# Value projections of a hybrid GLA/mLSTM layer with the weights held and the tokens streamed, turned back through a DRAM scratch

## The chip, the cores and the metric

The kernel runs on one core of a Trainium2 chip. The metric is the device time of one execution in microseconds (us), the median of three runs. The profile is that of one execution. TensorE (PE in the profile) multiplies: it holds a stationary tile of 128 x 128 and streams columns of the moving operand past it; VectorE (DVE), ScalarE (ACT) and GpSimd (POOL) work on tiles in on-chip memory; SyncE (SP) issues most DMA transfers, in the order of its program.

## The reference, cut to what matters

One decoder layer on 1024 tokens of width 1024, with 16 meta tokens ahead of them. The mixing block projects the normed tokens, runs four GLA heads and four mLSTM heads in chunks of the sequence, and merges the two; a gated, convolved FFN follows. The change touches `g_v` and `m_v`, the values of the heads: 1040 tokens x 256 columns for each head.

```python
proj = h @ w_in + b_in
g_q, g_k, g_v, g_r, g_lr, m_q, m_k, m_v, m_o, ... = split(proj)
# per head and chunk, GLA:
out   = (q * exp(bc)) @ S + scores @ vc
S_new = exp(b_last) * S + (k * exp(b_last - bc)).T @ vc
# mLSTM: num = w_inter * (qc @ C) + qk @ vc ; C_new = g_prev * C + (w_state * k).T @ vc
```

## The kernel before, in words

**Precision and tiles.** The normed tokens lie in on-chip memory with the model dimension on the partitions, as `xH` and `xL` (128 x 8 blocks x 1040 tokens each; rounded part and remainder). Each weight unit comes from DRAM as a raw tile `wr_*` by a SyncE DMA (`prep`, L131 to L148) and is split into `wH_*` (ScalarE copy, L146) and `wL_*` (VectorE subtract, L147). Two raw tiles and three pairs of split ones are there at a time, so a weight load waits until an earlier raw tile has been split. The split is held behind a named instruction (`hold`), so that it doesn't come ahead of an eviction. A product is three matmuls per block of 128: H x H, H x L, L x H.

**Keys, queries and merge gates** (`proj_cm`, matmul L234) hold the weights and stream tokens, in thirds of some 346 columns (342 for gates), and leave output columns on the partitions and tokens along the free dimension.

**Values** (`value_proj`, `proj_v`, L247 to L281) are wanted the other way round: `vt` (128 x 9 x 257) has tokens on the partitions, one group for the meta tokens and one for each of the eight chunks of 128. So the tokens are the stationary operand, and the weights stream, 256 columns at a time; a head's weights come as two units of four blocks x 256 columns (1 KB runs). Each head has nine PSUM tiles `pv` (of the ring `pj`, three banks, which keys, queries and gates use too): the meta tile, 16 matmuls with the packed `xM` (meta columns of `xH` and `xL` side by side, L263), joined by a ScalarE copy (L268) and VectorE adds (L269, L270); then eight chunks of 24 matmuls (L276), each evicted by one VectorE add of a bias spread over the partitions, `bB` (L280; loaded per head by SyncE, L598).

**Who uses `vt`.** In `gla` (heads 0 to 3) and `mlstm` (4 to 7): the states `u` (L1004, L1128) and `up` (L997, L1124), the meta output `omp` (L1014, L1140), and the output `op` (L1038, L1156). `up{s}_{c}` uses chunk c+1 of `vt` (for GLA, pairs of chunks). When a head is done, `post` scales and turns its output by VectorE block transposes (L750) into tiles `of` of the ring `r` (two buffers) and stores them by SyncE in four pieces each to the scratch `oscg` or `oscm` (L760).

**The order of the work.** `main` (L1193) walks the projections of the heads as generators, and after each step lets the side work (the attention of the head before, `gla(s)` or `mlstm(s)`, then `post`) go on by 1.15 steps: key and query of head 0, then for each head s its values, then the keys and queries of head s+1. A value projection has nine steps. Behind the last head come three merge gates (units gb0 to gb2, tiles pj33 to pj35), during which head 7 is finished; then two more gates (gb3, gb4, tiles `pc`) on other banks, and then the gate products `Vg`, `Xg`, `Yg`, `Zg` (L1222), with operands from `TL`, tiles that SyncE loads from the scratch `tsc` (L1337) behind the stores of head 7. `gw00`, `gw10` and so on are weights for later. A scheduler with priorities turns the program's order into an order for each engine; that is fixed when the kernel is built.

## Time and profile before

| | |
|---|---|
| median of three runs | 1838.67 us (1837.76 to 1839.79) |
| the profiled execution: its time, its span | 1838.8 us, 1837.1 us |
| granted TensorE clock | 0.998 |
| busy: TensorE, VectorE, ScalarE, GpSimd | 1820.4, 1243.0, 850.6, 442.7 us |
| value projections on TensorE start at | 67.0, 122.3, 189, 254.2, 321.4, 377.5, 441.9, 512.7 us |
| end of the last value projection, of head 7 | 542.1, 564.3 us |

How to read it: the span is from the first to the last instruction of the profiled execution. A row of a group ends in "xcount | busy us, mean ns of one | idle time of the engine just before them, and what ended most of it". A row of the chain has its start, its duration, the engine, the tile's name without its number, the line and the count. The profile names lines of the kernel before; those of the kernel after are a few to some twenty higher.

### The profile page before, as it was taken

The numbers are of one execution on the slowest core, as the hardware profiler recorded it, in microseconds if no ns is written. First come the engines' busy times: TensorE is split into PE (matmuls) and PEld (weight loads), VectorE is DVE, ScalarE is ACT, GpSimd is POOL, SyncE is SP. The second block draws the span as 40 slices with busy tenths as digits, with TensorE's granted clock in tenths as the row PEclk, the third lists the DMA queues.
The fourth block names the chain that finished last, engine by engine and source line by source line (L and its number), as shares of the span: only waits on it lengthen the run. The fifth ranks groups of instructions, "written<-read, shape, count | busy, mean of one in ns | idle before, by whom it ended". The sixth has DMA issues, their size and how long they took to land.

```text
span 1837.1 us, 32479 instructions
## 1 busy us (share of the span) xinstructions
PE 1820.4 (99%) x13142; PEld 1754.7 (96%) x13142; DVE 1243.0 (68%) x1858; ACT 850.6 (46%) x1366; POOL 442.7 (24%) x511
## 2 busy tenths in 40 slices
PE   8999999999999999999999999999999999999998
PEld 7999999999999999999999999999999999988876
DVE  7966856656553666764614537798878887787776
ACT  6564564645444433422512335544434434465664
POOL 6400211105530011134462710022222222200010
PEclk9999999999999999999999999999999999999999
DMA  5211212224436354566964743344333343398794
GB/s 164 59 48 52 55 31 61 57 74 141 127 81 180 87 169 152 161 186 197 341 195 130 255 143 128 106 125 121 104 110 109 105 129 114 98 340 314 279 381 163
DMA packets 237469, 269.63 MB, mean 147 GB/s; under 512 B 15282, under 2 KB 194797, under 8 KB 237319
## 3 DMA queue, kind: packets, MB, share of 16 engines
q1 hardware_dynamic: 215583, 196.20, 34.3%
q0 software_dynamic: 19136, 62.62, 9.9%
q10 hardware_dynamic: 2600, 8.74, 1.3%
q8 instruction: 103, 1.69, 0.4%
q14 instruction: 47, 0.39, 0.1%
HBM read 197.91 MB, written 69.60 MB: 146 GB/s over the span
## 4 chain that ended last, share of the span: by engine, by line
PE 87%; DVE 6%; DMA 3%; ACT 2%; issue 2%; POOL 1%; SPq 0%; POOLq 0%; DVEq 0%; ACTq 0%
PE pj L234 10%; PE pv L276 8%; PE Yu L1222 7%; PE Zu L1222 7%; PE Xu L1222 7%; PE bg L1475 5%; PE bm L1475 5%; PE Zg L1222 4%; PE Yg L1222 4%; PE Xg L1222 4%; PE po L1769 4%; PE Vu L1222 3%; PE pdZ L1925 2%; PE pdX L1925 2%; PE pdY L1925 2%; PE Vg L1222 2%
## 5 line engine op out<-in xcount | busy, mean ns | idle before, releaser
L657 POOL TENSOR_TENSOR ts<-ts 128x256 f32<-128x256 f32 x88 | 80.0, 916 | 47.9 <-DMA ts<-in_ffn_w_down_dram 46.1
L1682 POOL TENSOR_TENSOR SB<-SA,rg 128x512 f32<-128x512 f32 x20 | 32.8, 1638 | 239.5 <-issue 101.4
L276 PE MATMUL pv<-wH_mv,xH 128*128 128x256 f32 x256 | 74.5, 291 | 0.1
L276 PE MATMUL pv<-wH_gv,xH 128*128 128x256 f32 x256 | 74.3, 290 | 0.0
L1769 PE MATMUL po<-wH_wo,yH 128*128 128x256 f32 x256 | 72.5, 283 | 0.1
L276 PE MATMUL pv<-wH_gv,xL 128*128 128x256 f32 x256 | 72.0, 281 | 0.0
L276 PE MATMUL pv<-wL_mv,xH 128*128 128x256 f32 x256 | 72.0, 281 | 0.0
L1769 PE MATMUL po<-wL_wo,yH 128*128 128x256 f32 x256 | 71.7, 281 | 0.3 <-DVE wL_wo L147 0.3
L276 PE MATMUL pv<-wL_gv,xH 128*128 128x256 f32 x256 | 71.9, 281 | 0.0
L276 PE MATMUL pv<-wH_mv,xL 128*128 128x256 f32 x256 | 71.9, 281 | 0.0
L1769 PE MATMUL po<-wH_wo,yL 128*128 128x256 f32 x256 | 71.8, 281 | 0.0
L1717 DVE SCALAR_TENSOR_TENSOR cv<-u,fc,cv 128x1024 f32<-128x1024 f32 x44 | 65.2, 1481 | 0.4
L1664 POOL TENSOR_TENSOR A<-u2raw,A 128x512 fp32r<-128x512 f32 x20 | 42.5, 2124 | 86.2 <-ACT A L1663 86.2
L924 POOL TENSOR_TENSOR pk<-pk,kT 128x256 f32<-128x256 f32 (+1 forms) x24 | 31.8, 1330 | 130.2 <-ACT pk L922 130.2
L1475 PE MATMUL bg<-ogL,wH_bg 128*128 128x342 f32 x192 | 61.5, 320 | 0.0
L1475 PE MATMUL bg<-ogH,wH_bg 128*128 128x342 f32 x192 | 61.5, 320 | 0.0
L1475 PE MATMUL bm<-omH,wH_bm 128*128 128x342 f32 x192 | 61.4, 320 | 0.0
L1475 PE MATMUL bm<-omH,wL_bm 128*128 128x342 f32 x192 | 61.3, 319 | 0.0
L1475 PE MATMUL bg<-ogH,wL_bg 128*128 128x342 f32 x192 | 61.3, 319 | 0.0
L1475 PE MATMUL bm<-omL,wH_bm 128*128 128x342 f32 x192 | 61.2, 319 | 0.0
L280 DVE TENSOR_TENSOR v<-pv,bB 128x256 f32<-128x256 f32 x64 | 26.6, 415 | 40.0 <-PE pv L276 39.8
L1663 ACT ACTIVATE HA<-rg 128x1024 fp32r<-128x1024 f32 x16 | 17.0, 1060 | 72.7 <-PE Yu L1222 72.3
(829 smaller groups left out, 7479.6 us busy)
## 6 DMA issues: line engine op xcount, KB each, us to landing
gw<-in_w_in_dram SPq DMA_DIRECT2D x26, 512.0 KB
ts<-in_ffn_w_down_dram POOLq DMA_DIRECT2D x44, 256.0 KB, 4.4
tdn<-ts POOLq DMA_DIRECT2D x44, 256.0 KB, 3.3
rg<-in_ffn_w_up_dram SPq DMA_DIRECT2D x22, 512.0 KB
ru<-in_ffn_w_up_dram SPq DMA_DIRECT2D x22, 512.0 KB
adr<-s SPq DMA_DIRECT2D x40, 256.0 KB
rd<-in_ffn_w_down_dram SPq DMA_DIRECT2D x20, 512.0 KB
do<-tdn SPq DMA_DIRECT2D x18, 512.0 KB
```

What stands on the lines that cost most here:

```text
L234: nc.tensor.matmul(pt[:, :n], a[:, k, :], b[:, k, base + t0:base + t0 + n], start=(i == 0), stop=(i == 3 * NK - 1))
L276: nc.tensor.matmul(pt[:, :DV], a[:, k, t0:t0 + P], b[:, k % 4, :], start=(i == 0), stop=(i == 3 * NK - 1))
L280: hold(nc.vector.tensor_tensor(vt[:n, c, :DV], pt[:n, :DV], bB[:n, :], OP.add).ins)
L657: nc.gpsimd.tensor_tensor(t[:, o], t[:, a], t[:, b], OP.subtract)
L924: eng.tensor_tensor(e, e, k, OP.mult)
L1222: nc.tensor.matmul(out[:, :n], x[:, k, :], y[:, k, :], start=start and k == 0 and j == 0, stop=stop and k == 3 and j == 2, skip_group_chec ...
L1475: nc.tensor.matmul(pt[:, i, :n], a[:, k, :], b[k][:, base + t0:base + t0 + n], start=(k == 0 and j == 0), stop=(k == NK - 1 and j == 2))
L1664: eng.tensor_tensor(l, src, h.bitcast(F32), OP.subtract)
L1682: late.tensor_tensor(sb[:, 0:4], sa[:, 0:4], rg[:, 0:4], OP.subtract)
L1717: nc.vector.scalar_tensor_tensor(y, u[:, j:SEQ + j], fc[:, j, jj:jj + 1], y, OP.mult, OP.add)
L1769: nc.tensor.matmul(pt[:, :DV], a, b[:, k % 4, :], start=(k == 0 and i == 0), stop=(k == NK - 1 and i == len(terms) - 1))
L1925: nc.tensor.matmul(banks[r, j, b][:, c], p, q[:, c], start=first and k == 0, stop=last and k == 2, skip_group_check=True)
```

## The change

Three things change in the values. First, `u_v` makes the weight units column halves: all eight blocks x 128 columns, in 512 B runs. Second, `proj_v` holds these weights and streams the tokens, meta ones included, in three segments of 400, 384 and 256 columns (`VSEG`), for each of the two halves; a head has six PSUM tiles of 24 matmuls each. Third, the result has output columns on the partitions, and is turned: ScalarE evicts it with the bias as a column (tile `vs`, two buffers), VectorE transposes it in 32 x 32 blocks into a tile `vr` of the ring `r`, which `post` uses as well; when both halves of a segment are there, SyncE stores it in four pieces (256 B runs) to a DRAM scratch `vsc`, and loads it from there into `vt` as token rows (1 KB runs). The load of a segment is put into the program after the first tile of the next segment; that of the last, at the first step of the next generator (`late_loads`). The number of steps of a head stays nine.

With it: the packed meta tile `xM`, its fill and two copies go; so do the `bB` loads; the biases of the values come as columns with the other small rows (two more `va` loads on GpSimd's queue). `hold` takes two instructions. The columns of a head's values stand in blocks of 32 in another order, which `post`'s transpose and `by_block` undo for the outputs.

```diff
-    def proj_v(us, bB, vt):
+    VSEG = [(0, 400), (400, 384), (784, 256)]
+    vsc = [dram.tile([1 + 4 * NC, 32, DV], F32, name=f"vsc{s}") for s in range(2 * H)]
+
+    def proj_v(s, us, c0, vt):
...
-                        nc.tensor.matmul(pt[:, :DV], xM[:, 48 * k:48 * k + P], b[:, k % 4, :],
-                                         start=(i == 0), stop=(i == 2 * NK - 1))
...
+        due_load = []
+        for g, (t0, n) in enumerate(VSEG):
+            nb, b0 = n // 32, 0 if g == 0 else 1 + (t0 - NM) // 32
+            at = 1 if g == 0 else 0
+            R = hd.tile([P, T], F32, name=f"vr{s}_{g}", tag="r", bufs=2)[:, :64 * (nb + at)].rearrange(
+                "p (b t j) -> p b t j", t=2, j=32)
+            for j in range(2):
+                wH, wL = U.got[us[j]]
+                pt = ps.tile([P, 512], F32, name=f"pv{us[j]}_{g}", tag="pj", bufs=3)
...
+                    for a, b in ((wH, xH), (wH, xL), (wL, xH)):
+                        nc.tensor.matmul(pt[:, :n], a[:, k, :], b[:, k, t0:t0 + n], start=(i == 0), stop=(i == 3 * NK - 1))
...
+                    S = hd.tile([P, 400], F32, name=f"vs{us[j]}_{g}", tag="vs", bufs=2)
+                    kept_ = nc.scalar.activation(S[:, :n], pt[:, :n], AF.Identity, bias=cc(c0 + j))
+                    if at:
+                        nc.vector.transpose(R[:, 0, j, :], S[:, :32])
+                    turned_ = nc.vector.transpose(R[:, at:, j, :], S[:, NM * at:n].rearrange("p (b j) -> p b j", j=32))
+                    hold(turned_.ins, kept_.ins)
+                if j == 0:
+                    for load in due_load:
+                        load()
+                    due_load.clear()
                 yield
...
-                nc.tensor.matmul(pt[:, :DV], a[:, k, t0:t0 + P], b[:, k % 4, :],
-                                     start=(i == 0), stop=(i == 3 * NK - 1))
-                hold(nc.vector.tensor_tensor(vt[:n, c, :DV], pt[:n, :DV], bB[:n, :], OP.add).ins)
+            for q in range(4):
+                nc.sync.dma_start(vsc[s][b0:b0 + nb + at, :, 64 * q:64 * q + 64].rearrange("b i w -> i b w"),
+                                  R[32 * q:32 * q + 32].rearrange("p b t j -> p b (t j)"))
+
+            def load(g=g, t0=t0, n=n):
+                c = 0 if g == 0 else (t0 - NM) // P
+                m = n // P
+                nc.sync.dma_start(vt[:, 1 + c:1 + c + m, :DV],
+                                  vsc[s][1 + 4 * c:1 + 4 * (c + m)].rearrange("(c b) i w -> (b i) c w", b=4))
+                if g == 0:
+                    nc.sync.dma_start(vt[:NM, 0, :DV], vsc[s][0, :NM, :])
+            due_load.append(load)
+        late_loads.extend(due_load)
...
     def u_v(n0, name):
-        return [U.add(wsrc(w_in, 4 * g, 4, n0, DV), [P, 4, DV], f"{name}{g}") for g in range(2)]
+        return [u_cm(w_in, n0 + P * j, f"{name}{j}") for j in range(2)]
...
     def main(gen, pace=PACE):
         for _ in gen:
+            for load in late_loads:
+                load()
+            late_loads.clear()
```

The order on the engines changes with it, in two places. The first is SyncE's queue around head 0's values and the weights of heads 1 and 2 (`wr_gq1` the query weights of head 1, `wr_gv1_0` and `wr_gv1_1` its value weights, `wr_gk2` and `wr_gq2` key and query of head 2). Before:

```order
L142 DMA wr_gq1_920<-in_w_in_dram 128x8x128
L142 DMA wr_gv1_0_1297<-in_w_in_dram 128x4x256
L142 DMA wr_gv1_1_1303<-in_w_in_dram 128x4x256
L598 DMA bB2_2114<-in_b_in_dram 128x256
L142 DMA wr_gk2_1454<-in_w_in_dram 128x8x128
L142 DMA wr_gq2_1817<-in_w_in_dram 128x8x128
L142 DMA wr_gv2_0_1823<-in_w_in_dram 128x4x256
```

Now:

```order
L148 DMA wr_gv1_0_1260<-in_w_in_dram 128x8x128
L148 DMA wr_gv1_1_1266<-in_w_in_dram 128x8x128
L293 DMA vsc0_100<-vr0_0_930 32x13x64 x4
L299 DMA v0_922<-vsc0_100 128x3x256
L302 DMA v0_922<-vsc0_100 16x256
L293 DMA vsc0_100<-vr0_1_1043 32x12x64 x4
L148 DMA wr_gk2_1416<-in_w_in_dram 128x8x128
L148 DMA wr_gq2_1738<-in_w_in_dram 128x8x128
L299 DMA v0_922<-vsc0_100 128x3x256
L293 DMA vsc0_100<-vr0_2_1159 32x8x64 x4
L299 DMA v0_922<-vsc0_100 128x2x256
L148 DMA wr_gv2_0_1744<-in_w_in_dram 128x8x128
```

The stores and loads of head 0's values now stand among the weight loads; the load of segment 1 (128x3x256, the second of its kind) is behind wr_gk2 and wr_gq2.

The second place is the end of the heads. On SyncE, before (`of7` are the turned outputs of head 7):

```order
L142 DMA wr_gb3_5900<-in_w_in_dram 128x8x128
L142 DMA wr_gb4_6007<-in_w_in_dram 128x8x128
L1280 DMA gw00_6150<-in_w_in_dram 128x8x128
L760 DMA oscm_423<-of7_0_6065 32x8x128
L743 DMA omdm_425<-om7_5718 2x256
L760 DMA oscm_423<-of7_0_6065 32x8x128 x3
L1280 DMA gw10_6151<-in_w_in_dram 128x8x128
L760 DMA oscm_423<-of7_1_6097 32x8x128 x4
L1337 DMA TL0_6123<-tsc258_430 128x4x258
```

Now:

```order
L148 DMA wr_gb3_5570<-in_w_in_dram 128x8x128
L148 DMA wr_gb4_5677<-in_w_in_dram 128x8x128
L781 DMA oscm_429<-of6_1_5279 32x8x128 x2
L1304 DMA gw00_5820<-in_w_in_dram 128x8x128
L293 DMA vsc7_107<-vr7_2_5304 32x8x64 x4
L299 DMA v7_5067<-vsc7_107 128x2x256
L1304 DMA gw10_5821<-in_w_in_dram 128x8x128
L781 DMA oscm_429<-of7_0_5735 32x8x128
L764 DMA omdm_431<-om7_5383 2x256
L781 DMA oscm_429<-of7_0_5735 32x8x128 x3
L781 DMA oscm_429<-of7_1_5767 32x8x128 x4
L1361 DMA TL0_5793<-tsc258_436 128x4x258
```

The last segment of head 7's values is stored and loaded behind wr_gb3, wr_gb4 and gw00, and the loads of TL stay behind the outputs of head 7.

TensorE at the same place, before (`pj33` is the first merge gate behind the heads, `pj34` the second, `pj35` the third; `op7_7` is the last output of head 7):

```order
L234 MATMUL pj33_684_5858<-xL_101,wH_gb0_5362 128x342
L234 MATMUL pj33_684_5858<-xH_100,wL_gb0_5363 128x342
L1156 MATMUL op7_6_5884<-v7_5357,wt7_5562 128x257
L1157 MATMUL op7_6_5884<-C7_5_5851,WB7_5440 128x257
L1156 MATMUL op7_7_5892<-v7_5357,wt7_5562 128x257
L1157 MATMUL op7_7_5892<-C7_6_5885,WB7_5440 128x257
L234 MATMUL pj34_0_5906<-xH_100,wH_gb1_5729 128x342
```

Now:

```order
L240 MATMUL pj35_342_5709<-xH_108,wL_gb2_5405 128x342
L1145 MATMUL up7_6_5519<-v7_5067,KT7_5281 128x257
L1177 MATMUL op7_6_5554<-v7_5067,wt7_5224 128x257
L1178 MATMUL op7_6_5554<-C7_5_5521,WB7_5133 128x257
L1177 MATMUL op7_7_5562<-v7_5067,wt7_5224 128x257
L1178 MATMUL op7_7_5562<-C7_6_5555,WB7_5133 128x257
L240 MATMUL pj35_342_5709<-xH_108,wH_gb2_5404 128x342
```

The last outputs of head 7 move from the end of gate pj33 into the third gate, pj35.

58 lines of the change are left out of this document (22 added, 36 removed).

## The prediction, on record before the result

> **What bounds the kernel now.** I read the page first: busy time by engine, and the chain that ended last by engine.
>
> ```profile
> PE 1820.4 (99%) x13142; PEld 1754.7 (96%) x13142; DVE 1243.0 (68%) x1858; ACT 850.6 (46%) x1366; POOL 442.7 (24%) x511
> PE 87%; DVE 6%; DMA 3%; ACT 2%; issue 2%; POOL 1%; SPq 0%; POOLq 0%; DVEq 0%; ACTq 0%
> ```
>
> TensorE (PE) is busy for 99% of the span, and 87% of the last chain is its. That is a mean, so I looked next at the windows view of the stretch that the change touches, the projections of the eight heads, and at head 0 in it.
>
> ```profile
> core 0: us, PE busy (x) PEld busy (x) DVE busy (x) ACT busy (x) POOL busy (x), PEclk, DMA share, GB/s
> 66.00:610.00 544.00, 542.54 (x3780) 524.55 (x3779) 334.38 (x550) 277.11 (x538) 116.33 (x122) 1.00 0.30 82
> 67.00:89.00 22.00, 21.79 (x178) 20.80 (x176) 21.19 (x36) 7.90 (x11) 10.49 (x6) 1.00 0.09 25
> ```
>
> In 544 us TensorE stands for 1.5 us. VectorE (DVE) is at 61%, ScalarE (ACT) at 51%, the DMA engines at 30%. So in this stretch a microsecond of matmul that goes is a microsecond of the kernel, as long as nothing takes TensorE's place. Only in head 0, from 67 to 89, is VectorE nearly as full as TensorE (21.19 of 22.00).
>
> **What the change does to TensorE.** The chain in order of time, around the last head and at the kernel's end, gives the price of a matmul by its streamed columns (start, duration, what).
>
> ```profile
> 512.74 1.88 PE pv L263 x16
> 516.35 17.04 PE pv L276 x144
> 542.12 0.43 PE u L1128 x2
> 563.88 0.43 PE op L1157 x2
> 564.32 22.60 PE pj L234 x144
> 612.37 1.45 PE Yg L1222 x12
> 1820.29 2.77 PE pdX L1925 x12
> ```
>
> 256 columns cost 17.04/144 = 118.3 ns (L276); the meta tile's, also 256, 1.88/16 = 117.5 (L263); 342 columns 22.60/144 = 156.9 (L234); 512 columns 2.77/12 = 230.8 (L1925). Before, a head takes 192 x 118.3 + 16 x 117.5 = 24.59 us. After, it has 48 matmuls each of 400, 384 and 256 columns. No row has 400 or 384; on the line between 342 and 512 columns (0.435 ns a column) they cost 182.1 and 175.2. The head then takes 48 x (182.1 + 175.2 + 118.3) = 22.83 us: 1.76 us less, **14.1 us less in eight heads**. Where it comes from: a fixed part of a matmul is paid 144 times a head, not 208, and the streamed columns go from 208 x 256 = 53248 to 48 x 1040 = 49920. At the 342-column row's price per column (0.459 ns) the saving is 13.2 us, at the 512-column row's (0.451 ns) 15.6. I take the line.
>
> [...]
>
> **The other engines.** The groups by line, VectorE, then ScalarE:
>
> ```profile
> L280 DVE TENSOR_TENSOR v<-pv,bB 128x256 f32<-128x256 f32 x64 | 26.6, 415 | 40.0 <-PE pv L276 39.8
> L270 DVE TENSOR_TENSOR v<-vlo,bB 16x256 f32<-16x256 f32 x8 | 4.0, 498 | 0.1
> L750 DVE STREAM_TRANSPOSE of<-or 128x1024 f32<-128x1024 f32 x16 | 19.6, 1233 | 4.6 <-ACT or L741 4.6
> L268 ACT ACTIVATE vlo<-pv 16x256 f32<-16x256 f32 x8 | 3.0, 375 | 0.2
> L593 ACT ACTIVATE qT<-pj,col 128x348 f32<-128x348 f32 x4 | 2.2, 552 | 9.7 <-PE pj L234 9.7
> L550 ACT ACTIVATE kT<-pj,col 128x256 f32<-128x256 f32 x6 | 2.8, 462 | 0.0
> L502 ACT ACTIVATE xM<-xH 128x128 fp32r<-128x128 f32 x1 | 0.3, 309 | 0.1
> ```
>
> VectorE loses 8 x 0.415 + 0.498 = 3.8 us a head, and another add of the meta tile. It gains eight block transposes over 2 x 1040 columns; at L750's 1.2 ns a column that is 2.5 us, with eight starts some 3 us. It is relieved a little. ScalarE gains six evictions a head: L593 and L550 lie on 0.462 + 1 ns x (columns - 256), so 2 x (0.61 + 0.59 + 0.46) = 3.3 us, less 0.375: 23 us in 544, half idle. Both are hidden behind TensorE while its banks are three deep. The packed copy of the meta columns (two of 0.3 us on ScalarE, L502) and eight bias loads go too; I count them at nothing, since no matmul stands behind them.
>
> Two bias loads more stand on GpSimd's queue at the start (start, duration; the second row is its next work on x):
>
> ```profile
> 12.89 0.52 POOL L473 DMA_DIRECT2D va<-in_ml_norm_dram  x1
> 16.55 1.92 POOL L414 TENSOR_TENSOR xr<-xv,mhalf 128x1 f32<-128x1 f32 x2 [2.15 <-DVE xv L412]
> ```
>
> Two times 0.52 us fit into the 2.15 us for which GpSimd waited on VectorE there: 0, and at most 1.
>
> **The way through DRAM.** The values now reach `vt` by four stores and a load per segment. No row shows this trip; the nearest are stores and loads of like shapes: KB of each, then median us from issue to landing; the SyncE (SP) issue of a store (min/median/max); and the queue's packets.
>
> ```profile
> tsc<-xa POOLq DMA_DIRECT2D x6, 129.0 KB, 5.7
> go<-oscm POOLq DMA_DIRECT2D x8, 512.0 KB, 5.3
> msc<-lrs POOLq DMA_DIRECT2D x1, 32.5 KB, 3.3
> L760 SPq DMA_DIRECT2D oscg<-of x32: 302/456/1013, 134.5 to 364.4; - x32
> q1 hardware_dynamic: 215583, 196.20, 34.3%
> ```
>
> Store 3.3 to 5.7, load about 5.3, issues 5 x 0.46: 9 to 13 us from the transposes to the values in `vt`. The stores are in pieces of 256 B. A packet of q1 took on the mean 0.343 x 16 x 1837.1 us / 215583 = 47 ns, and the first segment's four stores have 128 x 13 = 1664 packets, 104 to an engine: 4.9 us if each costs that much, inside the 5.7.
>
> Who waits? A head's values are used first by the `u` and `up` matmuls behind its projection, and segment 1's (chunks 3 to 5) later still. Between heads the next head's key and query projections lie ahead of most of these: cost 0 for heads 1 to 6. **Head 0** is the tight one. Its chain in order of time, and SyncE's issues there:
>
> ```profile
> 88.24 0.64 ACT kq L834
> 88.93 0.50 PE sc L841
> 89.42 0.23 PE pv L276 x2
> 90.77 0.71 PE pv L276 x6
> 91.71 1.89 PE pv L276 x16
> 94.50 2.84 PE pv L276 x24
> 98.65 2.84 PE pv L276 x24
> 101.97 3.77 PE pj L234 x24
> 110.80 0.43 PE omp L1014 x2
> 103.11 0.37 SPq L142 DMA_DIRECT2D wr_gk<-in_w_in_dram  x1
> 104.25 0.37 SPq L142 DMA_DIRECT2D wr_gq<-in_w_in_dram  x1
> ```
>
> By the order of SyncE, the load of head 0's segment 1 stands behind wr_gk2 and wr_gq2, and those, before, were issued only at 103.11 and 104.25, when VectorE's splits let buffers go, 2.8 us after the projection's end at 98.65 + 2.84 = 101.49. With one SyncE issue more and the eviction now in two steps I put the load at +3 to +4.5, landed 5.3 later: +8.3 to +10, and +13 if contention adds 3. The order of TensorE needs it in the second half of `up0_1`, before at 110.80 + 3 x 0.43 - 101.49 = +10.6. So a wait of 0 to 5 us (it can slide as SyncE catches up); **I take 1.5**, nearer the end that the 5.3 us row gives, with something for the queue of stores behind it.
>
> Also in head 0, up to 88.93 TensorE follows VectorE and ScalarE (the `kq` product that ends at 88.88). Behind that point lie 2 + 6 + 16 + 24 + 24 = 72 matmuls, 8.5 us; of the head's 1.76 us the share ahead of it, (24.59 - 8.5)/24.59, **1.2 us, is lost** to that chain; at best nothing is, as VectorE has less to do.
>
> **Head 7** is the other. Its last segment's stores stand on SyncE behind wr_gb3, wr_gb4 and gw00, and `up7_6` moves from gate 33 into gate 35. From the end of the projection, E, TensorE reaches the end of gate 33 at 11 x 0.43 + 72 x 0.157 = 16.0 us, when the split that frees gw00 can run; then split, issues, stores and load, 12 to 15 us: in `vt` at E + 28 to 31. `up7_6` comes at 16.0 + 102 x 0.157 + 9 x 0.43 = E + 35.9: no wait. But head 7 now ends at E + 38.1 instead of 564.31 - 542.12 = E + 22, and behind it come its norm, its stores and, on SyncE, the loads of TL:
>
> ```profile
> 580.90 8.70 SPq L1337 DMA_DIRECT2D TL<-tsc  x8
> ```
>
> Before, the last was issued at 589.6, E + 47.5; 16 us later is E + 63.4, landed at E + 69. The matmuls that need them (Yg, L1222) come at 612.37 - 542.12 = E + 70.3. The slack shrinks from about 17 us to 1: wait 0 to 3, taken as 0.
>
> **The sum**, against the profiled execution's 1838.8 us (span 1837.1; the median of three runs is 1838.67, 0.1 away): -14.1 + 1.2 + 1.5 = -11.4. From the median: **1827.3 us**. With every unknown at its best end (-15.6, no waits, nothing lost) 1823.1.
>
> **The rivals.**
>
> *Part of the gain goes into waits.* Head 0 waits 5 us and TL 3 us: -14.1 + 1.2 + 5 + 3 = -4.9, 1833.8. For it: the small distances above, and stores of 256 B, four times as many packets as the 1 KB loads of the same bytes. [...] If a store's packet costs twice the mean, 9.8 us for the first segment, head 0's load of that segment would be late as well as that of segment 1, and that is this case. Against it: DMA share 0.09 to 0.30 in the stretch. Chance 0.18.
>
> *No gain.* The 400-column matmuls cost per column what the 256-column ones do (118.3/256 = 0.462 ns): a head is then 49920 x 0.462 = 23.06 us, 1.5 us saved still, 12.2 in all; so only waits of some 10 us make it none. 1838; chance 0.06.
>
> *Slower.* The transposed tile `R` has two buffers, shared with the transposed outputs (`of`). A third tile waits until the stores out of an earlier one have landed. SyncE issues in order, so a store can stand behind a load of the scratch (a wait of 5 us) or a weight load that itself waits for a split on VectorE; VectorE then stands at the transpose, with the next splits and the evictions behind it. TensorE is ahead by two banks, 2 x 24 x 182 ns = 8.7 us. With `of` in the ring, a wait is stores 5.7 + a load's wait 5.3 + issues 1.8 = 12.8, over the lead by 4.1 us; in seven heads 29 us: 1838.7 - 11.4 + 29 = 1856; once in two heads, 1842. It decides from a VectorE wait of 8.7 us. For it: VectorE at 96% in head 0, and SyncE's rows with loads between stores. Against it: VectorE has 39% to spare over the stretch, the tiles of a head are 8 us apart. Chance 0.12.
>
> **How the numbers follow.** The forecast has 0.64, the rivals 0.18, 0.06 and 0.12. The range reaches from the best end 1823.0 over the forecast and the partial case to 1835.0 and leaves 0.18 out. A measurement tells 0.2%, 3.7 us, from no change, so the partial case is still faster: 0.82 faster, 0.06 same, 0.12 slower.
>
> **What would show it.** In the profile after: matmuls of 400 and 384 columns at 182 and 175 ns by the chain; eight fewer and shorter value projections, 22.8 us each; TensorE idle in the heads' stretch 1.5 to 5 us, all of it in head 0, behind a DMA of `v`; Yg with no wait; VectorE busy a few us less, ScalarE some 23 more; the transposes never waiting on a store for over 8 us. I am wrong if TensorE waits on transposes, on `vt` in heads 1 to 6, or if a matmul of 400 columns takes over 190 ns.

## The result, and the profile after

The changed kernel takes 1850.05 us in the median (1848.36 to 1854.23, 4 runs), the old one beside it 1838.22: a ratio of 1.0066, 95% interval 1.0048 to 1.0085. It is slower by some 12 us where 11.4 less were forecast. The profiled execution took 1848.4 us, with a span of 1846.6. One run of all those below, of e11, took 2957 us at a granted clock of 0.556; the intervals leave it out.

The page of the kernel after, busy time by engine; then its windows, for the stretch of the heads, for head 0 at its start, for head 1, and for 6 us inside head 1 (the columns are those of the windows shown before the result):

```profile
PE 1811.9 (98%) x12630; PEld 1742.0 (94%) x12630; DVE 1244.2 (67%) x1842; ACT 869.7 (47%) x1406; POOL 443.2 (24%) x512
```

```profile
66.00:610.00 544.00, 534.48 (x3280) 513.21 (x3280) 335.81 (x537) 297.74 (x579) 116.97 (x122) 1.00 0.41 108
67.00:89.00 22.00, 20.38 (x126) 18.81 (x124) 21.14 (x35) 9.54 (x13) 12.03 (x6) 1.00 0.20 50
122.00:189.00 67.00, 64.63 (x397) 62.40 (x396) 47.23 (x74) 38.68 (x76) 8.69 (x8) 0.97 0.33 80
150.00:156.00 6.00, 6.00 (x40) 6.00 (x39) 6.00 (x9) 1.94 (x3) 1.33 (x2) 0.72 0.27 85
```

TensorE now stands for 9.5 us of 544, not 1.5. VectorE has as much to do as before (335.81 against 334.38), so "relieved a little" was wrong, if not by much; but it hasn't become the bound by its sum either. From 150 to 156 it is full (6.00 of 6.00), and the clock granted to TensorE is 0.72 there.

What TensorE waits for, in the kernel after (sum, times, longest; the waits of the program's start, `xtp`, `idlea`, are in the old kernel as well):

```profile
PE Yg L1246 <- DVE gu L1282: 3.7, 3, 1.6
...
PE sc L893 <- DVE pk L946: 2.4, 1, 2.4
PE bm L1499 <- DVE yg L1535: 2.2, 1, 2.2
PE pj L240 <- ACT vs L282: 1.6, 1, 1.6
...
PE sc L862 <- ACT kq L855: 1.4, 3, 0.9
PE sct L882 <- DVE A L912: 1.2, 2, 0.7
```

None of it is a wait for `v`. The waits are of two places: `sc`, `sct` and `pj` lie in the heads, `Yg` and `bm` behind them, in the gate stage and the merge, where the change has no instruction. So the table below cuts the span at the first matmul of each part. For the old kernel and the changed one (start of the first value matmul, of the first of head 4, of the gate stage, of the merge's `bg` and `bm`):

```profile
67.09 0.28 PE L263 MATMUL pv<-wH_gv,xM 128*128 128x256 f32 x1
...
321.37 0.47 PE L263 MATMUL pv<-wH_mv,xM 128*128 128x256 f32 x1
...
609.35 0.28 PE L1222 MATMUL Vg<-xH,gHA 128*128 128x258 f32 x1
...
880.81 0.32 PE L1475 MATMUL bg<-ogH,wH_bg 128*128 128x342 f32 x1
...
971.63 0.32 PE L1475 MATMUL bm<-omH,wH_bm 128*128 128x342 f32 x1
```

```profile
68.79 0.34 PE L278 MATMUL pv<-xH,wH_gv 128*128 128x400 f32 x1
...
324.66 0.54 PE L278 MATMUL pv<-xH,wH_mv 128*128 128x400 f32 x1
...
609.56 0.28 PE L1246 MATMUL Vg<-xH,gHA 128*128 128x258 f32 x1
...
888.26 0.32 PE L1499 MATMUL bg<-ogH,wH_bg 128*128 128x342 f32 x1
...
980.99 0.39 PE L1499 MATMUL bm<-omH,wH_bm 128*128 128x342 f32 x1 [2.21 <-DVE yg L1535]
```

| part of the span, us | before | forecast | after |
|---|---|---|---|
| start, to the first value matmul | 67.1 | 67.1 | 68.8 |
| GLA heads 0 to 3 | 254.3 | | 255.9 |
| heads 4 to 7, up to the gate stage | 288.0 | | 284.9 |
| all heads | 542.3 | 530.9 | 540.8 |
| gate stage, Vg to bg | 271.5 | 271.5 | 278.7 |
| bg to bm | 90.8 | 90.8 | 92.7 |
| bm to the end | 865.5 | 865.5 | 865.6 |

The heads gave 1.5 us where 11.4 were forecast, and 10.8 us were lost in parts that the forecast left as they were: 1.7 at the start, 7.2 and 1.9 behind the heads. The GLA heads are even longer than before; all that was gained came from the mLSTM heads.

### The profile page after: what moved, and what is told of

Read it like the earlier page. It is cut to its first block, busy times and chain, and to the rows that moved or that the text cites. A ratio compares the mean times of both kernels' runs of the same rounds, so it can differ in the third digit from the quotient of the medians.

```text
span 1846.6 us, 31681 instructions
## 1 busy us (share of the span) xinstructions
PE 1811.9 (98%) x12630; PEld 1742.0 (94%) x12630; DVE 1244.2 (67%) x1842; ACT 869.7 (47%) x1406; POOL 443.2 (24%) x512
## 4 chain that ended last, share of the span: by engine, by line
PE 55%; DMA 4%; DVE 3%; issue 1%; POOL 1%; ACT 0%; POOLq 0%; DVEq 0%; ACTq 0%
PE Yu L1246 6%; PE Zu L1246 6%; PE Xu L1246 6%; PE bm L1499 5%; PE bg L1499 5%; PE po L1793 4%; PE pdX L1949 3%; PE pdZ L1949 3%; PE pdY L1949 3%; PE Vu L1246 3%; PE Yg L1246 2%; PE Zg L1246 2%; PE Xg L1246 2%; PE pdV L1949 2%; DMA go<-omdm 1%
## 5 line engine op out<-in xcount | busy, mean ns | idle before, releaser
L278 PE MATMUL pv<-xH,wH_gv 128*128 128x400 f32 (+2 forms) x192 | 65.1, 339 | 0.0
L278 PE MATMUL pv<-xH,wH_mv 128*128 128x400 f32 (+2 forms) x192 | 64.6, 337 | 0.0
L278 PE MATMUL pv<-xL,wH_gv 128*128 128x400 f32 (+2 forms) x192 | 62.5, 325 | 0.0
L278 PE MATMUL pv<-xH,wL_gv 128*128 128x400 f32 (+2 forms) x192 | 62.3, 324 | 0.0
L278 PE MATMUL pv<-xL,wH_mv 128*128 128x400 f32 (+2 forms) x192 | 62.0, 323 | 0.0
L278 PE MATMUL pv<-xH,wL_mv 128*128 128x400 f32 (+2 forms) x192 | 61.5, 320 | 0.0
L1275 ACT ACTIVATE u2raw<-Xu 128x258 f32<-128x258 f32 (+1 forms) x44 | 16.5, 374 | 69.3 <-PE Xu L1246 69.3
L1793 PEld LDWEIGHTS po<-wH_wo,yH 128*128 128x128 f32 x256 | 48.1, 188 | 0.6 <-DVE h L1800 0.3
```

Source lines behind the costliest of these rows:

```text
L278: nc.tensor.matmul(pt[:, :n], a[:, k, :], b[:, k, t0:t0 + n], start=(i == 0), stop=(i == 3 * NK - 1))
L1275: evicted["U"] = nc.scalar.activation(u2, X[:, :n], AF.Copy).ins
L1793: nc.tensor.matmul(pt[:, :DV], a, b[:, k % 4, :], start=(k == 0 and i == 0), stop=(k == NK - 1 and i == len(terms) - 1))
```

## The experiments

All times are medians in us; the ratio is to the old kernel, run on the same chip; the parts are those of the table above, each from the profiled run's first matmuls.

| kernel | time (range, runs) | ratio, 95% interval | start | heads | Vg to bg | bg to bm |
|---|---|---|---|---|---|---|
| e1 bias loads elsewhere | 1844.9 (1843.4 to 1847.3, 5) | 1.0033, 1.0020 to 1.0045 | 65.7 | 541.2 | 277.3 | 90.9 |
| e2 tail on another queue | 1842.3 (1838.1 to 1849.7, 11) | 1.0022, 1.0010 to 1.0034 | 68.8 | 539.3 | 274.2 | 92.2 |
| e3 no trip | 1841.6 (1840.7 to 1844.1, 10) | 1.0019, 1.0010 to 1.0028 | 74.0 | 539.1 | 272.2 | 90.3 |
| e4 no trip, no transposes | 1833.2 (1830.9 to 1834.4, 5) | 0.9966, 0.9953 to 0.9979 | 75.4 | 529.4 | 272.2 | 90.3 |
| e5 short transposes | 1828.3 (1827.7 to 1829.7, 4) | 0.9945, 0.9931 to 0.9958 | 69.2 | 529.9 | 272.2 | 90.4 |
| e6 turned out of PSUM | 1839.4 (1838.1 to 1844.3, 10) | 1.0004, 0.9992 to 1.0015 | 68.5 | 540.3 | 274.1 | 91.0 |
| e7 three repairs | 1842.3 (1837.7 to 1848.6, 11) | 1.0017, 1.0006 to 1.0028 | 66.6 | 542.9 | 272.4 | 93.2 |
| e8 four segments | 1842.3 (1840.0 to 1849.5, 8) | 1.0026, 1.0015 to 1.0037 | 67.7 | 541.4 | 273.8 | 90.8 |
| e9 old kernel, padded | 1843.2 (1838.7 to 1846.7, 12) | 1.0022, 1.0012 to 1.0031 | 67.6 | 542.3 | 276.5 | 90.8 |
| e10 two scratches | 1847.1 (1844.0 to 1849.2, 5) | 1.0043, 1.0031 to 1.0055 | 69.5 | 541.7 | 278.2 | 90.4 |
| e11 splits on GpSimd | 1841.1 (1838.5 to 1843.1, and one of 2957; 11) | 1.0011, 1.0002 to 1.0019 | 66.9 | 542.2 | 273.9 | 90.4 |
| e12 old addresses | 1843.2 (1842.2 to 1846.8, 8) | 1.0029, 1.0019 to 1.0039 | 68.4 | 543.9 | 272.2 | 90.4 |
| e13 and the tail | 1845.2 (1841.0 to 1847.4, 5) | 1.0035, 1.0023 to 1.0048 | 69.0 | 547.8 | 272.2 | 90.4 |
| e14 all repairs | 1839.7 (1837.6 to 1842.6, 11) | 1.0007, 0.9998 to 1.0016 | 66.8 | 543.1 | 272.2 | 90.4 |
| e15 mLSTM heads alone | 1837.8 (1837.1 to 1839.5, 11) | 0.9997, 0.9988 to 1.0005 | 66.7 | 542.1 | 272.2 | 90.4 |
| e16 old addresses, early | 1840.5 (1837.9 to 1843.8, 11) | 1.0006, 0.9997 to 1.0015 | 68.5 | 542.4 | 272.2 | 90.4 |
| e17 all repairs, early | 1836.5 (1834.8 to 1839.9, 11) | 0.9989, 0.9980 to 0.9998 | 66.4 | 538.9 | 272.2 | 90.4 |
| e18 mLSTM heads, early | 1835.6 (1834.8 to 1838.5, 11) | 0.9983, 0.9975 to 0.9992 | 66.9 | 538.6 | 272.2 | 90.3 |

### The start and the tail: e1, e2

The rows that ask for e1: GpSimd's queue at the start, and the ScalarE copy behind it, in the kernel after. The second bias load holds back `lrs` (0.99 us of waiting), and ScalarE waits 3.46 us for it, where it waited 0.80 in the old kernel, with the evictions of `xH` queued behind.

```profile
15.48 0.51 POOL L176 DMA_DIRECT2D lrs<-in_gla_b_gate_dram  x1 [0.99 <-DMA va<-in_b_in_dram]
...
20.95 1.06 ACT L202 ACTIVATE wgp<-lrs 17x384 fp32r<-17x384 f32 x2 [3.46 <-DMA lrs<-in_gla_b_gate_dram]
```

**e1** gives these two loads to ScalarE's queue.

```diff
+    for dst, ap in small[9:11]:
+        with tc.issue_after(sent.ins):
+            nc.scalar.dma_start(dst, ap)
-        for dst, ap in small[4:11]:
+        for dst, ap in small[4:9]:
```

> The two bias loads of the values are issued by ScalarE at the start instead of by GpSimd; nothing else moves on any engine. Theory A (the start costs 1.7 us because the two loads on GpSimd's queue delay the gate-weight load lrs, for which ScalarE stands 3.5 us): the first value matmul starts at 67.1 us and not 68.8, and the time falls by 1.5 to 2 us, to about 1848.3. Rival (head 0 is bounded by VectorE anyway, so an earlier start is given back there): the first value matmul is earlier, but head 1 begins no earlier and the time stays at 1850.

The start is 3.1 us shorter, more than the 1.7 that it had lost, and the time falls by 5.1, more than the 2 expected. The loss at the start is shown. The other 2 us lie elsewhere: in the profiled executions the gate stage is 1.4 and the stretch from bg to bm 1.8 us shorter, the heads and the end 1.4 longer.

**e2** takes head 7's last stores and load from SyncE's queue, where they stand behind `gw00`:

```diff
-                nc.sync.dma_start(vsc[s][b0:b0 + nb + at, :, 64 * q:64 * q + 64].rearrange("b i w -> i b w"),
+                (nc.gpsimd if s == 7 and g == 2 else nc.sync).dma_start(vsc[s][b0:b0 + nb + at, :, 64 * q:64 * q + 64]...
-                nc.sync.dma_start(vt[:, 1 + c:1 + c + m, :DV],
+                (nc.gpsimd if s == 7 and g == 2 else nc.sync).dma_start(vt[:, 1 + c:1 + c + m, :DV],
```

> The stores and the load of the last segment of head 7 are issued by GpSimd instead of SyncE, so they no longer stand behind wr_gb3, wr_gb4 and gw00; the last output of head 7 moves from gate pj35 to gate pj34. Theory B (the gate stage loses 7 to 9 us because head 7 ends 16 us later, and its norm, the TL loads and the gate weights behind them run late into a loop of loads and products that cannot catch up): head 7's last output ends some 10 us earlier than in the changed kernel, TensorE's waits for gu in the gate products fall from 5 us to under 2, and the time is 1842 to 1845. Rival (the gate stage is slower for another reason, as memory traffic): the head ends earlier, the gate products still end 7 us late, 1849 to 1851.

Head 7 ends at E + 28.7, not E + 38.3, and the median falls by 7.8 us, but the runs now lie 11.6 us apart. The time is the one that theory B expects, but the gate stage has 274.2 us, still 2.7 over the old kernel. Of what is lost behind the heads, this does not tell how much is the tail's; e12 does.

### The trip or the turn: e3 to e6

**e3** leaves out the trip: no stores and no loads, and `vt` filled with 0.5 by GpSimd, so that the values used are not the right ones. **e4** leaves out the transposes too.

```diff
-            for q in range(4):
-                nc.sync.dma_start(vsc[s]...
-            def load(g=g, t0=t0, n=n):
...
+            nc.gpsimd.memset(vt, 0.5)
```

and in e4, besides:

```diff
-                    if at:
-                        nc.vector.transpose(R[:, 0, j, :], S[:, :32])
-                    turned_ = nc.vector.transpose(R[:, at:, j, :], S[:, NM * at:n].rearrange("p (b j) -> p b j", j=32))
-                    hold(turned_.ins, kept_.ins)
+                    hold(kept_.ins)
```

> Leaves out the stores to the scratch and the loads from it (the values are a constant); the matmuls, ScalarE's evictions and VectorE's transposes stay. Theory C (the waits in the heads come from the trip through memory: the ring of two tiles, SyncE's queue, traffic): TensorE stands under 2 us from the first to the last value matmul, these lie 463 us apart instead of 473, the tail is as before, and the time is 1828 to 1831. Rival D (the waits come from the order of ScalarE and VectorE, in which evictions and transposes stand among the steps of the attention): TensorE still stands 6 to 9 us there, and only the tail comes back, 1839 to 1843.

> As the one before, and VectorE's transposes are left out as well; matmuls and ScalarE's evictions stay. Theory D in its VectorE form (the transposes delay the attention's products): TensorE stands under 2 us in the heads, 1828 to 1831, while the kernel without the trip alone does not get there. Rival E (it is ScalarE's evictions, or the attention's own chain, that TensorE now runs into): it still stands 6 us or more, 1839 to 1843.

The fill costs some 5 us at the start in both (74.0 and 75.4), so the heads are compared: 539.1 without the trip, 540.8 with it; 529.4 without the transposes. The trip is worth 1.7 us, all but 0.1 of it in heads 4 to 7; VectorE's transposes are worth 9.7. The gate stage is 272.2 in both. That could be the tail, which is early here, or the scratches `vsc`, which a program without the trip doesn't have; it stayed open until e9.

**e5** keeps every instruction of the turn but makes the large transposes 32 columns wide, leaves out the stores, and loads `vt` from x and the meta tokens, so the values are others:

```diff
-                    turned_ = nc.vector.transpose(R[:, at:, j, :], S[:, NM * at:n].rearrange("p (b j) -> p b j", j=32))
+                    turned_ = nc.vector.transpose(R[:, at, j, :], S[:, NM * at:NM * at + 32])
```

> Each large transpose turns only its first 32 columns (0.2 us in place of 0.4 to 0.54), at the same place of VectorE's order and behind the same eviction; the stores to the scratch are left out and the loads take other data (rows of x), so nothing waits for the trip. Theory D1 (the time that the transposes take on VectorE is what the attention's products wait for): first to last value matmul 462 to 465 us, TensorE stands under 4 us there, 1832 to 1836. Rival D2 (it is their place, in order behind ScalarE's evictions, whatever they take): 470 to 473 us as with the full transposes, 8 us of waits, 1839 to 1842.

The heads take 529.9 us and the kernel 1828.27, below the 1832 to 1836 expected, as the gate stage is at 272.2 here too. That this is close to the forecast's 530.9 and 1827.3 is in part luck: the heads gave 1.0 us more than forecast, and the start took 2.1 more. Start of the first value matmul, and of head 4, in e5:

```profile
69.21 0.34 PE L278 MATMUL pv<-xH,wH_gv 128*128 128x400 f32 x1
...
316.32 0.54 PE L278 MATMUL pv<-xH,wH_mv 128*128 128x400 f32 x1
```

So the GLA heads take 247.1 us, 7.2 less than before: half of the 14.1 that the matmuls save, as it should be for four heads of eight. With the transposes at full width the same heads take 255.9, and 255.8 without the trip (e3): **8.8 us, and all of the gain of these heads, go with the time of VectorE's transposes**. TensorE stands for 6.5 us in these heads in the kernel after and for 1.0 in e5, and a stretch at half clock takes 1.7 more (last section). Here is how, in head 1 of the kernel after. VectorE first:

```profile
144.69 0.57 DVE L285 STREAM_TRANSPOSE vr<-vs 128x384 f32<-128x384 f32 x1
145.18 0.66 DVE L912 COPY_PREDICATED A<-mu,sc 128x512 f32<-128x512 uint8 x1
145.76 0.67 DVE L942 TENSOR_TENSOR pk<-bc 128x512 f32<-128x512 f32 x1
...
147.55 0.42 DVE L945 TENSOR_TENSOR pk<-pk,kT 128x256 f32<-128x256 f32 x1
147.89 2.89 DVE L946 TENSOR_TENSOR pk<-pk,qT 128x512 f32<-128x512 f32 x2
```

and TensorE:

```profile
145.84 1.05 PE L893 MATMUL sc<-pk 128*128 128x128 f32 x8
...
149.26 1.13 PE L893 MATMUL sc<-pk 128*128 128x128 f32 x8 [2.37 <-DVE pk L946]
```

From 139 to 150 VectorE has no gap. The product `pk`, for which TensorE waits, comes when VectorE's row has got to it, and the transposes stand in that row. The first of the two L946, which ends at 149.1, is the one that TensorE waits for; it took 1.22 us where the median of its line is 0.69, so not all of the wait is transposes (the old kernel has such slow ones too, up to 1.78). The head was close to two bounds, and only one was moved. Theory D1 holds in this: with the transposes at the same place but short, the loss is gone.

**e6** transposes straight out of PSUM, without ScalarE's eviction and the bias, to see whether the eviction's step in between makes the delay:

```diff
-                    S = hd.tile([P, 400], F32, name=f"vs{us[j]}_{g}", tag="vs", bufs=2)
-                    kept_ = nc.scalar.activation(S[:, :n], pt[:, :n], AF.Identity, bias=cc(c0 + j))
+                        nc.vector.transpose(R[:, 0, j, :], pt[:, :32])
+                    turned_ = nc.vector.transpose(R[:, at:, j, :], pt[:, NM * at:n].rearrange(...
```

> Leaves out the bias of the values: VectorE transposes straight out of the matmul's bank and ScalarE's eviction goes; the trip through the scratch and the tail stay as in the changed kernel. D1 (VectorE's time): VectorE's transposes take as long or longer, the heads stay at 471 to 474 us, 1848 to 1851. D2 (the two steps one behind the other): the heads fall to 462 to 466 us with waits under 4 us, 1839 to 1844.

The heads stay at 540.3 us, but two changes cancel in that. Start of the first value matmul, and of head 4, in e6:

```profile
68.50 0.34 PE L278 MATMUL pv<-xH,wH_gv 128*128 128x400 f32 x1
...
319.37 0.53 PE L278 MATMUL pv<-xH,wH_mv 128*128 128x400 f32 x1
```

The GLA heads take 250.9 us, 5.0 less than in the kernel after, though VectorE is as busy in them (177.3 us, after 177.7) and a large transpose takes as long (median 541 ns, after 535); the wait at 149 us is gone. Heads 4 to 7 take 289.5, 4.6 more: there TensorE waits once for 3.2 us for a ScalarE eviction (`kT`), and a stretch at half clock takes 1.7. So D2 does not fall. VectorE's time is not the whole of it: in the GLA heads the step on ScalarE ahead of the transposes is worth up to 5.0 of the 8.8 us, presumably because the transposes can start earlier without it. The time of the transposes and, by e6, the step ahead of them both count there.

### Three that did not help: e7, e8, e11

**e7** joins e1, e2, a ring of its own for head 7's last two tiles, and one transpose in place of two for the first segment (padded to 416 columns):

```diff
+            w, tg = (T + 3, "qk"[g - 1]) if s == 7 and g else (T, "r")
...
+                        nc.gpsimd.memset(S[:, :NM], 0.0)
+                    kept_ = nc.scalar.activation(S[:, NM * at:], pt[:, :n], AF.Identity, bias=cc(c0 + j))
+                    turned_ = nc.vector.transpose(R[:, :, j, :], S.rearrange("p (b j) -> p b j", j=32))
```

> The whole computation, with three repairs of the changed kernel: the bias loads on ScalarE's queue, the stores and load of head 7's last segment on GpSimd's queue with its turned tiles in buffers of their own, and one transpose instead of two for a tile with meta tokens (48 transposes, not 64). If the parts add (start -5.2, tail -7.7, some 3 us less VectorE work worth 0 to 2): 1835 to 1838, at or just under the kernel before. If the gate stage's loss has one cause that the first repair had already removed half of: 1839 to 1842.

No better than e2 alone: the parts did not add. The gate stage has no wait here (272.4 us), but the heads are 2.1 us longer than in the kernel after, as TensorE now waits 1.8 us for `v` in head 7, and bg to bm has 93.2.

**e8** cuts the tokens in four segments, for shorter bursts on VectorE at the price of more matmuls:

```diff
-    VSEG = [(0, 400), (400, 384), (784, 256)]
+    VSEG = [(0, 272), (272, 256), (528, 256), (784, 256)]
```

> Four segments of 272, 256, 256 and 256 columns instead of three (eight tiles a head, ten transposes, still nine steps). The matmuls of a head take 23.1 us instead of 22.8. If coarse tiles are what the attention's steps stumble over, the waits in the heads fall from 9 to under 5 us and the time to 1843 to 1847. If VectorE's time decides (its transposes get some 3 us longer over all the heads), or neither, 1850 to 1855.

The heads take 541.4, no less, and TensorE waits 9.1 us in them, 9.5 in the kernel after. The time, 1842.3, lies under both cases, by the gate stage (273.8).

**e11** (the padded segment, e1 and e2 with it) gives the splits of four heads' value weights to GpSimd:

```diff
-            parted[:] = [nc.vector.tensor_tensor(wL, raw, wH.bitcast(F32), OP.subtract).ins]
+            eng = nc.gpsimd if name[:3] in ("gv1", "gv2", "gv3", "mv0") else nc.vector
+            parted[:] = [eng.tensor_tensor(wL, raw, wH.bitcast(F32), OP.subtract).ins]
```

> The whole computation: the repaired kernel (bias loads on ScalarE, head 7's last segment on GpSimd's queue in the shared ring, one transpose per tile), and the splits of eight value weight tiles (heads 1 to 4, 1.22 us each on VectorE) moved to GpSimd. D1 (VectorE's time in the GLA heads is what TensorE waits for): 2.4 us a head come off VectorE, heads 1 to 3 fall by 1 to 3 us each against the repaired kernel, first to last value matmul 467 to 470 us, 1834 to 1838. If GpSimd's own products of the attention are delayed by the splits (some 4 us each): no gain or a loss, 473 us or more, 1842 or more.

The heads take 542.2 us, and TensorE waits 10.2 us in the GLA heads, not 6.5, though VectorE has 7.7 us less to do there (170.1, after 177.7). Among its waits are 4.3 us for VectorE's `A`, 1.8 for `pk` and 1.4 for `v`. So it is not enough to take work from VectorE. That what now waits for GpSimd makes the difference is a guess; it was not tried.

### What is lost behind the heads: e9, e10, e12 to e16

The gate stage's operands `go` are loaded by GpSimd's queue from the scratches `oscg` and `oscm`, and its results stored to `otdg` and `otdm`. DMA issues, KB and median us from issue to landing, before and after:

```profile
otdg<-gu POOLq DMA_DIRECT2D x8, 513.0 KB, 4.5
otdm<-gu POOLq DMA_DIRECT2D x8, 513.0 KB, 4.5
...
go<-oscg POOLq DMA_DIRECT2D x8, 512.0 KB, 4.8
```

```profile
otdg<-gu POOLq DMA_DIRECT2D x8, 513.0 KB, 5.8
otdm<-gu POOLq DMA_DIRECT2D x8, 513.0 KB, 6.3
...
go<-oscg POOLq DMA_DIRECT2D x8, 512.0 KB, 5.5
```

The same transfers of the same size are 15 to 40% slower, in a stage that the change doesn't touch. What is different, by the program, is the order of the scratches: the eight `vsc` (8.65 MB in all) are declared, and most of them first used, ahead of other scratches. That those then lie elsewhere is the author's inference: the profile shows no addresses, and "the old addresses" below means that the other scratches come in the old kernel's order, with `vsc` behind them.

**e9** is the old kernel with eight such scratches that nobody reads; a 32-byte store touches each:

```diff
+    pad = [dram.tile([1 + 4 * NC, 32, DV], F32, name=f"pad{s}") for s in range(2 * H)]
...
+    for s in range(2 * H):
+        nc.sync.dma_start(pad[s][0, :1, :8], ident[:1, :8])
```

> The kernel before with eight more scratch tensors in DRAM of the same size and at the same place in the allocation as the changed kernel's (8.65 MB), each touched by one store of 32 bytes; the work is the kernel before's. Theory G1 (where the later scratch tensors lie in memory makes the loads of the heads' outputs in the gate stage slower: 4096-byte packets 290 ns in the mean in the changed kernel, 204 before): the packets go to 250 to 290 ns here too, TensorE waits on the gate products for 3 to 5 us, 1841 to 1844. G2 (it is the timing of the changed kernel, not the place): 200 to 210 ns, no waits, 1838.5.

The old kernel, with none of its instructions changed (eight small stores come in at 29 to 31 us, and a few instructions between 23 and 37 us change places), takes 1843.19 us, 4.5 more, and scatters over 8 us. Its parts up to the heads' end are the old ones; the gate stage has 276.5:

```profile
609.93 0.28 PE L1224 MATMUL Vg<-xH,gHA 128*128 128x258 f32 x1
...
886.38 0.32 PE L1477 MATMUL bg<-ogH,wH_bg 128*128 128x342 f32 x1
```

**e10** has two scratches in place of eight, used in turn:

```diff
-    vsc = [dram.tile([1 + 4 * NC, 32, DV], F32, name=f"vsc{s}") for s in range(2 * H)]
+    vsc = [dram.tile([1 + 4 * NC, 32, DV], F32, name=f"vsc{s}") for s in range(2)] * H
```

> The changed kernel with two scratch tensors that the heads take in turn, in place of eight; the order on all engines is the same. G1 (place): other addresses for all that is allocated behind, the 4096-byte packets come down from 290 towards 205 ns and the time by 3 to 6 us, to 1844 to 1847. G2 (timing): packets and time stay, 1849 to 1851.

3 us less, the packets at 233 ns, and the gate stage hardly shorter (278.2): fewer bytes do not give the old addresses back, and they did not help much.

**e12** does: the other scratches are declared ahead of `vsc`, and 14 touching stores in the old kernel's order of first use stand ahead of the first value store. **e13** has e2's tail with it, **e14** all repairs (e12, e1, e2, and e7's padded segment).

```diff
+    osc = {g: dram.tile([NK, P, SEQ], F32, name=f"osc{g}") for g in "gm"}
+    omd = {g: dram.tile([H, 2, DV], F32, name=f"omd{g}") for g in "gm"}
...
+    adr = [dram.tile([NP2, 2, P, n, 256], F32, name=f"adr{i}") for i, n in enumerate((4, 3))]
     vsc = [dram.tile([1 + 4 * NC, 32, DV], F32, name=f"vsc{s}") for s in range(2 * H)]
...
+            for d in (osc["g"][0], omd["g"][0], rsc[0], osc["m"][0], omd["m"][0], tdn[0][0, :, 0], tdn[1][0, :, 0], gsc["b"][0],
+                      otd["g"][0], otd["m"][0], gsc["a"][0], hsc[0], adr[0][0, 0, :, 0], adr[1][0, 0, :, 0]) if s == g == 0 else ():
+                nc.sync.dma_start(d[:1, :8], msc[:1, :8])
```

> The changed kernel, with one thing added: as soon as the gate's scratch is written, 14 stores of 32 bytes touch the other DRAM scratches in the order in which the old kernel first uses them. [...] The instructions of the four compute engines keep their order. Theory G1 (where the scratches lie costs some 4.5 us from the heads' end on, as the old kernel with unused scratches put in between showed): the 4096-byte packets of the loads on GpSimd's queue come back from 290 ns to about 205, the stretch from the first Vg matmul to the first bg matmul from 278.7 to about 274, the heads stay at 473 us, and the time is 1844.5 to 1846.5. Rival T1 (the late end of head 7 alone makes the loss behind the heads): the packets may change, the time stays at 1849 to 1851.

> As the kernel with the old addresses, and the last segment's stores and load of head 7 are on GpSimd's queue. If placement and the tail are two separate losses (G1 and T1 both): op7_7 ends near E+29 in place of E+38, the gate stage waits 1 us or less, and the time is 2 to 4 us under that of the kernel with the old addresses alone, 1841 to 1843. If the tail costs nothing once the transfers are quick: the time of the kernel with the old addresses, within 1 us.

> The whole computation with every repair: the old addresses, the tail on GpSimd's queue, the two bias loads on ScalarE's queue at the start, and the first segment padded to 416 columns so that one transpose does for it. What is left of the loss is then only VectorE's time in the heads (waits of some 8 us and a stretch at half clock). If the parts add up: 1836 to 1839, level with the old kernel. If the repairs overlap, as they did in the kernel with three repairs (1842.3): 1840 to 1843.

The gate stage is back at 272.2 us, in all three; the mean of the 4096-byte packets of GpSimd's queue in the 110 us from Vg + 60 on is back at 201, 185 and 194 ns (before 204, after 291). e12's head 7 ends as late as the changed kernel's, so the late tail costs nothing behind the heads: T1 fell, and e13, with the tail mended, gained nothing by it (1845.2, neither the sum nor e12's time within 1 us; its five runs lie 6.4 us apart, and the heads of the profiled one, 547.8 us, have stretches at half clock that cost 6.8). e14, 1839.7, lies between its two cases. The heads of e12 are 3 us longer: the touching stores stand ahead of a weight load on SyncE's queue, which issues at 67.17, not at 62.60; ScalarE's copy waits for it, the evictions behind it too, and TensorE waits 4.1 us at 90 us (`sct`).

**e15** has the change in heads 4 to 7 alone, with e14's repairs; `proj_old` is the old `proj_v`.

```diff
+        if s < 4:
+            bB = hd.tile([P, DV], F32, name=f"bB{s}", tag="vs", bufs=1)
+            nc.sync.dma_start(bB, rowb(b_in, (O_GV if s < 4 else O_MV) + DV * (s % 4), DV))
+            yield from proj_old(uv[s], bB, vt)
+            return
```

> The change in heads 4 to 7 alone, heads 0 to 3 as in the old kernel; with the old addresses, the tail on GpSimd's queue, and the padded first segment; the eviction's buffers are one apiece for the two channel tiles. Theory D1 (VectorE, at 68 to 72 % busy in the GLA heads before the change, is what takes the gain; the mLSTM heads keep theirs): heads 0 to 3 take the old 254.3 us, heads 4 to 7 216 to 218 in place of 220.7, and with the tail mended 1834.5 to 1837.5, faster than the old kernel. Rival (the turn costs the mLSTM heads as much as it saves, or the tail takes it): 1838 to 1842.

1837.78, no different from the old kernel and 0.3 us above the range of D1, with the touching stores' wait in it: heads 0 to 3 take 257.5 us, not 254.3.

**e16, e17 and e18** are e12, e14 and e15 with the touching stores some 30 us earlier, where SyncE's queue is empty; three more (`tsc`, `msc`) go ahead, so that the old order stays.

```diff
+                for d in (tsc[0][0, :, 0], tsc[1][0, :, 0], msc, osc["g"][0], omd["g"][0], ...
+                    nc.sync.dma_start(d[:1, :8], ident[:1, :8])
```

> The changed kernel with every scratch but the value scratches at the old kernel's address, as in the first kernel with the old addresses, but the touching stores (now 17) stand on SyncE's queue some 30 us earlier, behind the small loads of the start and ahead of the token sums' stores, where the queue was empty. In the first one they stood ahead of the load of the second query tile, which issued at 67.2 us in place of 62.6, and TensorE waited 4.1 us at 90 us. Theory G2 (that wait was the touches' own cost): the wait is back at under 1 us, the heads wait 9 us as in the changed kernel, the first Vg to the first bg stays at 272 us, and the time is 1839.5 to 1841.5: placement is worth 9 to 10 us. Rival (the wait at 90 us belongs to something else): 1842.5 to 1844.

> All repairs, with the touching stores early. By G2 the 4.1 us wait in head 0 goes and 3 us with it: 1836 to 1837.5, a little under the old kernel. Rival: 1839 to 1840.5, as with the touches late.

> The change in heads 4 to 7 alone, with the touching stores early. There the load of the second query tile was late as well (ScalarE stood 5.8 us on it, and TensorE waited 1.5 us for the first value bank at 74 us and 1.0 us for a gate product at 92 us). By G2: 1835 to 1836.8, faster than the old kernel by some 0.1 %. Rival (the mLSTM heads alone have no more to give): 1837.3 to 1838.5.

All three came out as G2 has it. e16 is the changed kernel, with its four compute engines' instructions in the same order; only the scratches come in another order, and 17 small stores are added. Its gate stage and its transfers:

```profile
610.96 0.28 PE L1253 MATMUL Vg<-xH,gHA 128*128 128x258 f32 x1
...
883.13 0.32 PE L1505 MATMUL bg<-ogH,wH_bg 128*128 128x342 f32 x1
```

```profile
otdg<-gu POOLq DMA_DIRECT2D x8, 513.0 KB, 4.2
otdm<-gu POOLq DMA_DIRECT2D x8, 513.0 KB, 4.3
...
go<-oscg POOLq DMA_DIRECT2D x8, 512.0 KB, 5.0
```

It takes 1840.53 us, 9.5 less than the changed kernel, and by its interval can't be told from the old one. The split holds over all kernels here. In the eleven that have the old order of scratches or make no use of `vsc` (before, e3 to e5, e12 to e18) TensorE has no wait in the gate stage, which takes 271.5 to 272.2 us, and the packets take 185 to 204 ns in the mean. In the nine with the new scratches ahead (after, e1, e2, e6 to e11) the stage takes 272.4 to 278.7 us and the packets 233 to 291 ns. e17 is 2.3 us under the old kernel, e18, **the best of all, 3.2 us** (0.9983, 0.9975 to 0.9992). Its first value matmul, and head 4's:

```profile
66.93 0.28 PE L331 MATMUL pv<-wH_gv,xM 128*128 128x256 f32 x1
...
321.36 0.54 PE L289 MATMUL pv<-xH,wH_mv 128*128 128x400 f32 x1
```

Its GLA heads take 254.4 us, as in the old kernel; what it gains is in heads 4 to 7 (284.2 us, before 288.0). VectorE was less full there: in the old kernel it is busy for 55% of these heads and for 69% of the GLA heads.

## Why the prediction was wrong

**The matmuls' saving was right.** A run of ten matmuls of 400 columns, first and last, and one of nine of 384, in the kernel after:

```profile
514.58 0.34 PE L278 MATMUL pv<-xL,wH_mv 128*128 128x400 f32 x1
...
516.40 0.34 PE L278 MATMUL pv<-xH,wL_mv 128*128 128x400 f32 x1
```

```profile
144.08 0.33 PE L278 MATMUL pv<-xH,wL_gv 128*128 128x384 f32 x1
...
145.66 0.34 PE L278 MATMUL pv<-xH,wL_gv 128*128 128x384 f32 x1
```

(516.40 - 514.58)/10 = 182.0 ns, forecast 182.1; (145.66 - 144.08)/9 = 175.6, forecast 175.2. And e5's GLA heads gave 7.2 us, half of 14.1 being 7.05.

**The step that failed** is "Both are hidden behind TensorE while its banks are three deep". It counted VectorE's busy time (about right: some 3 us of transposes a head, and as much of adds gone) and not what stands behind the transposes in VectorE's row. TensorE's banks hide a late eviction of the values, but `pk`, `kq` and `A` of the head before are not values, and TensorE needs them at fixed places of its order. It cost 8.8 us in the GLA heads (e5 against after) and 9.2 to 9.7 in all heads (e3 less e5, e3 less e4). For ScalarE too the step is not quite right: in the kernel after and in e5 TensorE waits once, for 1.6 and 1.5 us in head 4, for an eviction `vs`. The profile of before had the sign of it, in a window that the prediction did not quote, head 1:

```profile
122.00:189.00 67.00, 66.05 (x468) 63.66 (x467) 46.26 (x77) 36.70 (x71) 8.51 (x8) 1.00 0.18 48
```

VectorE has 46.26 of 67 us there, 69%, and TensorE 1 us to spare. The prediction took the mean of 61% over all heads for VectorE's spare time, and feared for VectorE only in head 0.

**Also wrong.** "Two times 0.52 us fit into the 2.15 us" at the start: 1.7 us, as the DMA issues behind them were counted on GpSimd's row and not through `lrs` to ScalarE's (e1). And no step spoke of the gate stage and the merge other than by TL: 7.2 + 1.9 us there, from the order of the scratches (e16: 0.7 and -0.5). The trace of before does not show it.

**Right in kind.** The trip is cheap: `v` is not waited for in the kernel after, and the partial rival did not come. The term of 1.5 us for head 0 was too many, and the 1.2 us there are not seen either, as e5's GLA heads gave their whole share. The trip's price is 1.7 us, in heads 4 to 7, where none was forecast (e3 against after). In the kernel after, the tile `vr` (ns min, median, max of the large transposes; then us from a store's issue to its landing):

```profile
L285 DVE STREAM_TRANSPOSE vr<-vs x48: 402/535/592, 79.8 to 551.8; 128x384 f32<-128x384 f32 x32, 128x256 f32<-128x256 f32 x16
...
DMA to landing us min/median/max: 1.9/2.5/7.1
```

The stores land in 2.5 us in the median, under the 3.3 to 5.7 taken, so their pieces of 256 B had no price that can be seen in it. The 33792 packets of 256 B in this trace took 19.8 ns each in the mean, not the 47 that the prediction took; the doubled price that the partial rival supposes isn't seen. The kernel came out slower, as one rival had it, but not in that rival's way: VectorE waited for the ring of `vr` for 5.3 us in all, in two waits, and the rival needed 8.7 in one. The tail: head 7 ended at E + 38.3 (forecast 38.1), and Yg waited for `gu` (3.7 us), not for TL.

```profile
599.58 7.07 SPq L1361 DMA_DIRECT2D TL<-tsc  x3
```

The last of these loads is issued at E + 64.5, forecast E + 63.4.

**The sum**, in the terms of the profiled executions: forecast -11.4; e5 has -12.4 in the heads; the turn gives back 9.2 (e3 - e5; 1.7 of it is a stretch at half clock in e3) and the trip 1.7 (after - e3), so -1.5 is left in the heads; +1.7 at the start, +7.2 and +1.9 behind the heads, +0.1 at the end: +9.4, and the spans differ by 1846.6 - 1837.1 = 9.5. In the medians placement is worth 9.5 us (after against e16). In e16's profiled execution the two parts behind the heads are 8.9 us shorter than in that of after, but the whole is 5.9 shorter, as its heads and its end take 1.6 more each.

**Open.** Why the new order of scratches is slower, and which scratch does it, was not tried; nor was whether it is the declarations or the touching stores of e12 that bring the old times back, or that this goes by addresses at all. The shift cost 4.5 us in the old kernel and 9.5 in the changed one, by places that need not be the same, and e2, e6, e7, e8 and e11, with the changed kernel's scratches, have a gate stage of 272 to 274 us, not 278.7, which also leaves open why e2 is 7.8 us quicker. So the time that a bad place costs is not one number. That the transposes on VectorE are what costs the time is shown by e4 and e5; how much of it is their length and how much the moment at which ScalarE lets them start is not told apart (e6 says that both count), and the way through VectorE's row is argued from one wait in the timeline.
